# The order of the out-projection products of a seven-product feed-forward block

## The chip, the core and the metric

The kernel runs on one core of a Trainium2 chip. The core's engines work side by side, each through its own stream of instructions in order: TensorE (PE in the profile, with its weight loads as PEld), VectorE (DVE), ScalarE (ACT), GpSimd (POOL) and SyncE (SP), which here only starts transfers. They wait for one another through semaphores. The metric is the device time of one execution in microseconds (us); before the change it was 1460.97 us, the median of three runs (1460.22, 1460.97, 1462.96).

## What is computed

One inference step of a streaming speech encoder with model width 1024, for a prompt of 512 frames and for 8 running streams with 16 new frames each; 640 columns in all. Layer 0 is a convolution module and a feed-forward block, layer 1 is attention over shared keys and values and a second feed-forward block. Everything is float32. The change lies in the feed-forward blocks alone:

```python
def swiglu_ffn(h, g, w_in, w_out):
    a, b = jnp.split(rms_norm(h, g) @ w_in, 2, axis=-1)
    return h + (jax.nn.silu(a) * b) @ w_out
...
for l in range(DEPTH):
    ...
    h = swiglu_ffn(h, norm_ffn[l], w_ffn_in[l], w_ffn_out[l])
```

The hidden width is 2816, that is 22 blocks of 128.

## The kernel before

**Three matmuls for one.** The kernel keeps float32 accuracy by splitting each operand into a rounded part and a residue: `put` (L370) lets ACT copy the value into the high part (L371) and then lets DVE subtract that from the value for the low part (L372). A product of a weight tile and a tile of activations is three matmuls (high by high, low by high, high by low), all issued at L439.

**Seven products for eight.** Both matrix products of the feed-forward block are further cut with the Strassen-Winograd scheme: a 2x2 block product is made of seven products of sums of blocks. The 640 columns are the two halves of 320 (`NH`). For the input projection, `seven` (L524) makes one hidden block with both its columns' halves: it reads weights with `w_seven` (L410), makes seven products, and `gate` (L472) multiplies SiLU of `a` with `b`. Two of its seven products are put off: the function returns `after`, and `after(0)`, `after(1)` run the last products and the block's two gates. `combined` (L488) turns the gates of two neighbouring blocks into the block sums that the output projection needs. The last of their four gates, that of `after(1)` of the second block, makes four of them, named after their product in the table below: `XT2`, `X22`, `XT3` and `XT4`. Each is a gate or a subtraction on DVE (L476, L479, L510, L518), then a copy on ACT, then a residue on DVE.

**Output stretches.** `out_chunk` (L555) is called three times in each of the two feed-forward blocks, after six hidden blocks each time. The six *output stretches* are counted here in order of time: 1 to 3 in layer 0, 4 to 6 in layer 1. A stretch adds six hidden blocks' part of the output to `h`. It has four output row pairs `u` (0 to 3), and seven products for each. A product is three steps of three matmuls, one step for each pair of hidden blocks that it sums over; the third step of products 6, 3, 7 and 4 needs what the very last gate makes. The table of products and their PSUM buffers, and what one call does, are these lines (L557 to L580):

```python
prod = {5: ("e", XT1, True, 1, 1), 1: ("a", X11, True, 0, 0),
        2: ("b", X21, True, 0, 0), 6: ("a", XT2, False, 1, 0),
        3: ("e", X22, False, 1, 0), 7: ("a", XT3, False, 1, 1),
        4: ("a", XT4, False, 0, 1)}
...
    with tc.issue_after(last[0]) if last else nullcontext():
        ins = product(pt, ws[u][x], list(zip(HH[x], HL[x])), first,
                      {"": None, "'": (0, 1), '"': (2,)}[part])
    last[:] = [ins.ins]
    ...
        nc.vector.tensor_tensor(out=hv, in0=hv, in1=pt, op=sub if row else add)
```

Products 1, 6, 7 and 4 of one row pair pile up, in this order, in one PSUM buffer (`a`), products 5 and 3 in another (`e`). After each of them DVE adds the buffer to `h` (L580), and the next product may write the buffer only after that addition has read it.

**The order** of the products is written out by hand in the string `QORD` (L65). A token is product number and row pair: `60` is product 6 of row pair 0. A prime (`60'`) stands for the first two steps, a double prime (`60"`) for the third step, which ends the product and is followed by the addition. `a0` and `a1` are `after(0)` and `after(1)`. `issue_after` keeps the products of PE in this order. The last two products of row pair 3, `73` and `43`, are put between the products of the next call of `seven`. Everything else (the cuts of weights, the gates, the additions) is put in order by the compiler's planner, from its own estimate of when each is ready; on DVE and ACT the planned order is then fixed.

**Weights.** `w_seven(..., True)` is called at the first product of each row pair: one transfer of 768 KB into one of two buffers `raw` (SP, L414), two smaller ones into `s` (POOL, L417 and L418, the second adds to the first), three sums on DVE (L422, L423, L425; L422 is the first that needs `raw`), and seven cuts with `put`, in the order XT1, X11, X21, XT2, X22, XT3, XT4. The cut weights go to eleven slots in turn, so that a cut waits for the product that used the weights cut eleven places before. The cut for product 6 of row pair 2 thus waits for product 4 of row pair 0 (`40`), that for product 1 of row pair 2 for `30`, that for product 2 of row pair 2 for `70`. A `raw` buffer is free when the last of its seven cuts is done, and the transfer of the next `seven` waits for that of row pair 2.

Of the kernel before, what the change touches and what calls it, by code (L numbers as in the profile page):

```python
# [61 lines left out]
X11, X21, XT2, XT1, XT3, XT4, X22 = range(7)  # L62
NCH, CW = 3, 6
HIX = {X11: 0, X21: 1, XT1: 2, XT2: 3, XT3: 4, X22: 5, XT4: 6}
QORD = """50' a0 a1 10' 50" 10" 20 60' 30' 51' 51" 11' 60" 30" 11" 21 70 61 31 40 52 71 12 22 41 62 32 53 72  # L65
          13 23 42 63 33"""
BO = "a0 s0 a1 s1 b0 b1 t0 n0 p0 c0 d0 t1 n1 c1 d1"
BL = "a0 o2 s0 a1 o2 s1 q2 t0 q2 n0 b0 q2 b1 q2 c0 q2 d0 t1 q2 n1 o2 c1 o2 d1 p0 o2"
# [14 lines left out]
def tile_trunk(ctx, tc, xT, vecs, hist, w_pw1, w_pw2, w_in0, w_out0, w_os0, w_in1, w_out1, w_os1,  # L83
# [249 lines left out]
    def ffn(l, w_in, w_out, w_os, tail, hf, lead=(), b0=None, last_sum=()):  # L333
# [221 lines left out]
        def out_chunk(c, HH, HL, after):  # L555
# [26 lines left out]
            last = []  # L582
            for t in QORD.split():
                if t[0] == "a":
# [1103 lines left out]
```

## Time and profile before

| What | Number |
|---|---|
| median of three runs | 1460.97 us |
| profiled execution, its device time | 1461.67 us |
| span in its profile, first to last instruction | 1459.5 us |
| matmuls in the span | 11022, of which 1512 are those of the output stretches |
| TensorE clock granted | 0.999 of full speed |

The profile is one execution, 0.70 us longer than the median. A row of the timeline begins with start and duration in microseconds and ends, where the engine sat idle before it, with that idle time and what ended it. Matmuls overlap: a matmul of 320 columns is shown with 0.31 us, and the next one starts 0.145 to 0.15 us after it started. The starts are therefore what to count with.

### The profile page before, as it was taken

Reading aid. Unit: us, or ns where it says so; the run is one execution under the profiler, and the core shown is the slowest. Engines: PE = TensorE matmul, PEld = TensorE weight load, DVE = VectorE, ACT = ScalarE, POOL = GpSimd, SP = SyncE. Lnnn points to the kernel's source line nnn. Section 1 sums busy time; section 2 is a strip of 40 time slices with the busy share of each in tenths; the row PEclk is TensorE's granted clock in tenths of the full one; section 3 lists DMA queues with packets and bytes.
Section 4 is the critical chain, followed back from the end, with each engine's and each line's share of the span. In section 5 each row is a group of like instructions: output and inputs, shape, how many; then the busy total and the mean of one; then the engine's idle time right before and its main releaser. Section 6 shows DMA issues by size and latency. Waiting matters only on the chain. (4 is left out here: it accounts for less than half of the span.)

```text
span 1459.5 us, 28220 instructions
## 1 busy us (share of the span) xinstructions
PE 1432.7 (98%) x11022; PEld 1369.1 (94%) x11022; DVE 1144.6 (78%) x2520; ACT 758.5 (52%) x1628; POOL 297.5 (20%) x349
## 2 busy tenths in 40 slices
PE   9999999999999999999999999999999999999998
PEld 8998799999999999999987898878999999999998
DVE  6789867988888888756768668577889788879855
ACT  4666554654554554545564355443554464555443
POOL 5699130011111111013222121011001111111101
PEclk9999999999999999999999999999999999999999
DMA  7267434044534444425556554452134543534522
GB/s 243 74 182 187 121 87 145 14 134 150 138 103 140 141 104 121 116 87 194 181 163 214 179 190 159 140 197 72 39 82 128 151 134 89 175 101 106 162 62 72
DMA packets 66932, 192.56 MB, mean 132 GB/s; under 512 B 12144, under 2 KB 30320, under 8 KB 58480
## 3 DMA queue, kind: packets, MB, share of 16 engines
q1 hardware_dynamic: 52432, 160.58, 33.5%
q0 software_dynamic: 13504, 29.37, 10.0%
q8 instruction: 86, 1.41, 0.4%
q10 hardware_dynamic: 864, 0.83, 0.2%
q14 instruction: 46, 0.38, 0.1%
HBM read 179.14 MB, written 11.61 MB: 131 GB/s over the span
## 5 line engine op out<-in xcount | busy, mean ns | idle before, releaser
L439 PE MATMUL mm<-XH,whi 128*128 128x320 f32 x896 | 276.4, 310 | 4.6 <-ACT t L451 4.2
L439 PE MATMUL mm<-XH,wlo 128*128 128x320 f32 x896 | 276.1, 309 | 0.0
L439 PE MATMUL mm<-XL,whi 128*128 128x320 f32 x896 | 273.9, 309 | 0.0
L371 ACT ACTIVATE whi<-raw 128x512 fp32r<-128x512 f32 (+2 forms) x280 | 168.5, 613 | 134.7 <-PE mm L439 113.5
L372 DVE TENSOR_TENSOR wlo<-raw,whi 128x512 fp32r<-128x512 f32 (+2 forms) x280 | 184.3, 667 | 23.4 <-ACT whi L371 21.6
L199 PE MATMUL mm<-xh,whi 128*128 128x320 f32 (+2 forms) x640 | 200.2, 314 | 1.1 <-ACT whi L164 0.8
L200 PE MATMUL mm<-xh,wlo 128*128 128x320 f32 (+2 forms) x640 | 198.2, 311 | 0.0
L201 PE MATMUL mm<-xl,whi 128*128 128x320 f32 (+2 forms) x640 | 195.9, 311 | 0.4 <-DVE xl L189 0.4
L439 PE MATMUL mm<-hid,whi 128*128 128x320 f32 x732 | 171.8, 310 | 2.7 <-DVE h L580 2.7
L439 PEld LDWEIGHTS mm<-XH,whi 128*128 128x128 f32 x896 | 167.8, 188 | 7.0 <-ACT t L451 6.3
L439 PEld LDWEIGHTS mm<-XH,wlo 128*128 128x128 f32 x896 | 168.2, 188 | 0.0
L439 PEld LDWEIGHTS mm<-XL,whi 128*128 128x128 f32 x896 | 167.6, 188 | 0.0
L439 PEld LDWEIGHTS mm<-hid,whi 128*128 128x128 f32 x732 | 125.1, 188 | 4.3 <-DVE h L580 4.3
L199 PEld LDWEIGHTS mm<-xh,whi 128*128 128x128 f32 x640 | 120.5, 188 | 4.4 <-ACT xh L187 1.5
L201 PEld LDWEIGHTS mm<-xl,whi 128*128 128x128 f32 x640 | 119.7, 188 | 1.2 <-DVE xl L189 0.8
L200 PEld LDWEIGHTS mm<-xh,wlo 128*128 128x128 f32 x640 | 120.5, 189 | 0.2
L439 PE MATMUL mm<-hid,wlo 128*128 128x320 f32 x366 | 113.0, 309 | 0.0
L439 PE MATMUL mm<-XH,shi 128*128 128x320 f32 x344 | 106.0, 309 | 1.1 <-ACT t L451 1.1
L439 PE MATMUL mm<-XH,slo 128*128 128x320 f32 x344 | 106.0, 308 | 0.0
L439 PE MATMUL mm<-XL,shi 128*128 128x320 f32 x344 | 105.6, 308 | 0.0
L841 POOL TENSOR_TENSOR ca<-ca,cvt 128x512 f32<-128x512 f32 x60 | 91.9, 1531 | 17.8 <-ACT cvt L838 11.2
L417 POOL DMA_DIRECT2D s<-in_w_in x38 | 22.1, 582 | 355.7 <-DVE wlo L372 142.2
(275 smaller groups left out, 3372.7 us busy)
## 6 DMA issues: line engine op xcount, KB each, us to landing
raw<-in_w_in SPq DMA_DIRECT2D x38, 1024.0 KB
s<-in_w_in POOLq DMA_DIRECT2D x76, 256.0 KB, 4.2
raw<-in_w_os SPq DMA_DIRECT2D x24, 768.0 KB
cache<-in_ck SPq DMA_DIRECT2D x32, 512.0 KB
cache<-in_cv SPq DMA_DIRECT2D x32, 512.0 KB
raw<-in_w_pw SPq DMA_DIRECT2D x11, 1024.0 KB
s<-in_w_os POOLq DMA_DIRECT2D x48, 192.0 KB, 3.7
raw<-in_w_kq SPq DMA_DIRECT2D x8, 1024.0 KB
```

Source lines behind the costliest of these rows:

```text
L199: nc.tensor.matmul(ps, wh, xh, start=(first and i == 0), stop=False)
L200: nc.tensor.matmul(ps, wl, xh, start=False, stop=False)
L201: end = nc.tensor.matmul(ps, wh, xl, start=False, stop=(stop and i == last))
L371: put_end[1] = nc.scalar.activation(out=hi, in_=src, func=AF.Copy).ins
L372: put_end[0] = nc.vector.tensor_tensor(out=lo, in0=src, in1=hi.bitcast(F32), op=sub).ins
L417: nc.gpsimd.dma_start(s1, src[:, 2 * n:3 * n])
L439: last = nc.tensor.matmul(pt, wt, v, start=(first and k == i == 0), stop=(k == n - 1 and i == 2), skip_group_check=True)
L841: nc.gpsimd.tensor_tensor(out=acc, in0=acc, in1=pr, op=ALU.add)
```

## The change

Only the string `QORD` changes. Both orders have the same 26 products (252 matmuls a stretch, with `73` and `43`), the same loads, cuts, gates and additions.

```diff
-QORD = """50' a0 a1 10' 50" 10" 20 60' 30' 51' 51" 11' 60" 30" 11" 21 70 61 31 40 52 71 12 22 41 62 32 53 72
+QORD = """50' a0 a1 10' 50" 10" 20 60' 30' 51' 60" 30" 51" 70 11 21 40 61 31 52 71 12 22 41 62 32 53 72
           13 23 42 63 33"""
```

The third steps `60"` and `30"`, which need what the last gate makes, now stand ahead of `51"` and `11'` (nine matmuls). `70` now stands ahead of all of `11` and of `21`, and is parted from `60"` by `30"` and `51"` (six matmuls) where it was parted by `30"`, `11"` and `21` (fifteen). `40` stands ahead of `61` and `31`, and is parted from `70` by 18 matmuls as before. Product `11` is no longer made in two parts. From `52` on, the order is the former one.

## The prediction

> **What bounds the kernel now.** I read the page first, then the idle time of the matmul line L439, then the timeline of each output stretch.
>
> ```profile
> PE 1432.7 (98%) x11022; PEld 1369.1 (94%) x11022; DVE 1144.6 (78%) x2520; ACT 758.5 (52%) x1628; POOL 297.5 (20%) x349
> L439 PE MATMUL mm<-hid,whi 128*128 128x320 f32 x732 | 171.8, 310 | 2.7 <-DVE h L580 2.7
> ```
>
> PE is busy for 98% of the span. The change keeps every matmul, so it can only move what PE waits for, and in the stretches that is little. The view of line L439 counts it over the whole kernel (weight loads and matmuls together, so a wait can stand twice):
>
> ```profile
>   ACT t L451: 13.1, 20
>   DVE h L580: 12.8, 18
> ```
>
> The waits for `t` come from `seven`, and the change leaves them. Those for `h` are products waiting for an addition. What such a wait costs shows in stretch 2, ahead of `72`:
>
> ```profile
> 462.12 0.31 PE L439 MATMUL mm<-hid,slo 128*128 128x320 f32 x1
> 462.27 0.31 PE L439 MATMUL mm<-hid,shi 128*128 128x320 f32 x1
> 463.56 0.41 PE L439 MATMUL mm<-hid,shi 128*128 128x320 f32 x1 [0.99 <-DVE h L580]
> 463.82 0.31 PE L439 MATMUL mm<-hid,slo 128*128 128x320 f32 x1
> ```
>
> Matmuls start 0.146 us apart (462.12 to 462.27). The waiting one starts 1.29 after its forerunner, 1.14 too late, and the next 0.26 after it, 0.11 too late. So the loss is 1.26, which is the idle time shown plus 0.27. I price the other waits the same way.
>
> **The change part by part.** Nothing is added or removed: no instruction, DMA or buffer. Three things move.
>
> *1. `60"` is asked for nine matmuls earlier: 9 x 0.146 = 1.31 us.* It needs XT2 of the last gate, and its third matmul needs XT2's residue, written by DVE. In each stretch I looked up when that residue is done and when the third matmul runs:
>
> ```profile
> 330.97 0.48 DVE L580 TENSOR_TENSOR h<-h,mm 128x320 f32<-128x320 f32 x1
> 331.36 1.29 DVE L372 TENSOR_TENSOR hid<-B,hid 128x320 fp32r<-128x320 f32 x3
> 331.90 0.41 PE L439 MATMUL mm<-hid,shi 128*128 128x320 f32 x1
> 443.04 0.89 DVE L372 TENSOR_TENSOR hid<-B,hid 128x320 fp32r<-128x320 f32 x2
> 443.84 0.48 DVE L580 TENSOR_TENSOR h<-h,mm 128x320 f32<-128x320 f32 x1
> 444.23 0.31 PE L439 MATMUL mm<-hid,whi 128*128 128x320 f32 x1
> 556.62 0.88 DVE L372 TENSOR_TENSOR hid<-B,hid 128x320 fp32r<-128x320 f32 x2
> 557.71 0.31 PE L439 MATMUL mm<-hid,whi 128*128 128x320 f32 x1
> 1113.96 0.48 DVE L580 TENSOR_TENSOR h<-h,mm 128x320 f32<-128x320 f32 x1
> 1114.36 1.29 DVE L372 TENSOR_TENSOR hid<-B,hid 128x320 fp32r<-128x320 f32 x3
> 1114.90 0.41 PE L439 MATMUL mm<-hid,shi 128*128 128x320 f32 x1
> 1226.56 0.88 DVE L372 TENSOR_TENSOR hid<-B,hid 128x320 fp32r<-128x320 f32 x2
> 1227.76 0.46 PE L439 MATMUL mm<-hid,whi 128*128 128x320 f32 x2
> 1338.25 0.89 DVE L372 TENSOR_TENSOR hid<-B,hid 128x320 fp32r<-128x320 f32 x2
> 1339.44 0.31 PE L439 MATMUL mm<-hid,whi 128*128 128x320 f32 x1
> ```
>
> The first residue of each merged row is XT2's, 0.48 to 0.49 long. In stretch 1 it ends at 331.85 and the matmul starts 0.05 later: it was waiting for it already. In stretch 2 it is ready at 443.04 + 0.49 + 0.05 = 443.58 and used at 444.23, a slack of 0.65. Asked for 1.31 earlier, the matmul waits 1.31 - 0.65 + 0.11 = 0.77. Stretch 3 has 0.56 slack, hence 0.86; stretch 6 has 0.65, hence 0.77; stretch 5 has 0.67, hence 0.75. In stretches 1 and 4 the whole 1.31 would be lost, but there the addition just ahead of the residue (330.97, 1113.96) is that of `51"`, which now comes later. The residue moves up by that row's 0.40 us start to start, so 0.91 each. Sum of the six: **+4.97 us**. Behind the waiting matmul stand `30"`, `51"` and all further products, since PE's order is fixed. If DVE keeps its old order in stretches 1 and 4 too, the sum is 5.8. If the planner moves XT2's residue ahead of a weight cut, it is less (third rival).
>
> *2. `70` follows `60"` after six matmuls, 0.87 us, in place of fifteen.* Both write buffer `a`, so the addition of `60"` must be done in between. After XT2's residue DVE has two more, 0.40 us each start to start, then can take the addition. In stretch 2: with `51"`'s addition gone (443.84), XT4's residue takes that place, the addition of `60"` runs 444.24 to 444.72, and `70` is wanted at 443.58 + 0.25 + 0.87 = 444.70. It waits 0.07 + 0.11 = 0.18. One weight cut ahead of the addition in some stretches would add about 0.5 there; none is in the way if the addition goes first. I take 0.25 a stretch: **+1.50 us**. The nearest pair of the old order is `10"` and `60'`, also in one buffer, nine matmuls apart:
>
> ```profile
> 327.29 0.42 PE L439 MATMUL mm<-hid,shi 128*128 128x320 f32 x1 [0.57 <-DVE h L580]
> 553.34 0.42 PE L439 MATMUL mm<-hid,whi 128*128 128x320 f32 x1 [0.31 <-DVE h L580]
> 1110.29 0.41 PE L439 MATMUL mm<-hid,shi 128*128 128x320 f32 x1 [0.99 <-DVE h L580]
> 439.23 0.48 DVE L580 TENSOR_TENSOR h<-h,mm 128x320 f32<-128x320 f32 x1
> ```
>
> Three stretches lose 0.84, 0.58 and 1.26 there. In stretch 2 the addition ends at 439.71 for a product wanted at 439.98, 0.22 in hand with the 0.05. With six matmuls instead of nine, 0.44 less room, this gives 1.28 + 1.02 + 1.70 and 0.33 for each of the three others: 5.0 us. That is the upper end; the lower is 0.
>
> The Trainium skill, Perfetto Trace Analysis, Optimizing Tensor Performance, says that independent matmul groups should rotate through PSUM banks so that one group's evacuation lies beside the next group's matmuls. It speaks against this move, which puts two products of one bank closer; taken by itself it would set the upper end just worked out, and the three rows agree with it in three stretches of six.
>
> *3. `40` is done 18 matmuls, 2.63 us, earlier against the end of the group (ahead of `52`).* The chain that hangs on it ends in the wait shown first:
>
> ```profile
> 451.71 0.46 PE L439 MATMUL mm<-hid,whi 128*128 128x320 f32 x2
> 452.05 0.94 ACT L371 ACTIVATE whi<-raw 128x384 fp32r<-128x384 f32 x2 [0.74 <-PE mm L439]
> 453.60 0.55 DVE L372 TENSOR_TENSOR wlo<-raw,whi 128x384 fp32r<-128x384 f32 x1
> 454.17 0.33 SPq L414 DMA_DIRECT2D raw<-in_w_in  x1
> 462.42 0.69 DVE L422 TENSOR_TENSOR raw<-raw 128x512 f32<-128x512 f32 x1 [2.34 <-DMA raw<-in_w_in]
> 463.03 0.48 DVE L580 TENSOR_TENSOR h<-h,mm 128x320 f32<-128x320 f32 x1
> ```
>
> The first row is the last matmul of `40`, ending 0.31 later at 452.02, with the first of `52`. ACT cuts the weights whose slot `40` held, DVE ends the row pair's last cut at 454.15, SP issues the next weights' transfer at 454.17. L422 waits for it on DVE for 2.34 us, and the addition of `62`, long ready, stands behind L422 at 463.03 with `72` behind it at 463.56. The other stretches that wait there:
>
> ```profile
> 350.68 0.42 PE L439 MATMUL mm<-hid,whi 128*128 128x320 f32 x1 [0.30 <-DVE h L580]
> 576.98 0.42 PE L439 MATMUL mm<-hid,whi 128*128 128x320 f32 x1 [0.92 <-DVE h L580]
> 1134.17 0.41 PE L439 MATMUL mm<-hid,whi 128*128 128x320 f32 x1 [0.25 <-DVE h L580]
> 1358.42 0.42 PE L439 MATMUL mm<-hid,whi 128*128 128x320 f32 x1 [0.63 <-DVE h L580]
> 1119.10 0.41 PE L439 MATMUL mm<-hid,whi 128*128 128x320 f32 x1 [0.27 <-DVE h L580]
> ```
>
> With 0.27 each, `72` costs 0.57, 1.26, 1.19, 0.52, 0 and 0.90: 4.44 us. In the new order PE reaches `72` about 1.0 us later by parts 1 and 2, and the transfer is issued up to 2.63 - 1.0 = 1.6 us sooner on the clock. In stretch 2 `72` is then wanted at 463.4 and its addition is done by 462. Even a transfer that lands no sooner leaves only 0.1 there. I take all **-4.44 us**. The last row is `61` of stretch 4, waiting for the addition of the first product; `61` now comes 18 matmuls later, so **-0.54 us**. What `61` and `31` release for row pair 3 comes 1.3 us later, but eight products, 10.5 us, lie between `61` and `53`, the first to need it.
>
> Sum: 4.97 + 1.50 - 4.44 - 0.54 = **+1.5 us**. The profiled execution, 1461.67, would be 1463.2; as it lies 0.7 above the median, I predict on the median: 1460.97 + 1.5 = **1462.5 us**. I count on 0.2% (2.9 us) as what a measurement tells from no change, so the forecast is within it.
>
> **The rivals.**
>
> *`70` takes over the wait (slower).* DVE reaches the addition of `60"` behind gate residues and weight cuts, as it reached that of `10"`. For it: the three rows of `60'`, and a DVE that is busy for 7.94 of 8.00 us from 444 on in stretch 2 (the first row under the last rival). Against: DVE is then past the gate. It decides once the addition ends over 0.3 us after `70` is wanted. With 5.0 in place of 1.5 the sum is +5.0: **1466.0**.
>
> *The transfer isn't earlier (slower).* If DVE's backlog holds the last cut so that the transfer moves with PE, the waits at `72` stay: 4.97 + 1.50 - 0.54 = +5.9, **1466.9**. Against: the 2.15 us from the end of `40` (452.02) to the issue are a plain chain, with `40` at its head.
>
> *The gate's residue comes sooner (faster).* DVE takes XT2's residue well after ACT's copy. If the planner puts it two places earlier in stretches 2, 3, 5 and 6, their front waits (3.15) vanish: -1.7, 1459.3. If `70` doesn't wait either, -3.2: **1457.8**. Against: nothing that DVE does before that residue gets later there, so the planner has no reason.
>
> *The clock gives way.* More short gaps could lower PE's clock.
>
> ```profile
> 444.00:452.00 8.00, 8.00 (x56) 8.00 (x55) 7.94 (x19) 3.52 (x7) 0.57 (x1) 1.00 0.34 118
> 429.00:475.00 46.00, 44.49 (x302) 43.96 (x301) 1.00 0.49 142
> ```
>
> Both rows are of the windows view, the first with busy time of all engines (PE, PEld, DVE 7.94 of 8.00, ACT, POOL), the second with that of L439 alone (PE, PEld); the granted clock stands third from the end. It is 1.00 across stretch 2, whose gaps reach 0.99 us. A product of nine at half speed after each of six gaps would add 6 x 1.31 = 7.9 to the sum: 1470.4. The Trainium skill, TensorE: Matmul & The Clock Gate, A second HAM failure mode, tells of a kernel whose micro-idles between matmul groups made the clock swing between half and full; the trace disagrees for gaps of this size.
>
> **How the numbers follow.** Forecast, with the milder third rival (within 0.2%): 0.56. `70` takes over 0.20, transfer not earlier 0.12, clock 0.01, others slower 0.01: slower 0.34. Third rival in full: faster 0.10. The range leaves out half of the faster case and about a tenth at the top: 1458.3 to 1467.0, which takes in both slower rivals.
>
> **What would show it.** Right: in all six stretches the third matmul of `60"` waits for a residue (L372), 0.8 to 0.9 us; no wait ahead of `72`; the transfer after `40` 1 to 2 us earlier; `61` of stretch 4 free. Wrong: `70` idle over 0.3 us behind L580; L422 still idle for over 2 us with an addition that PE needs behind it; or XT2's residue at another place in DVE's order, which would change every term of part 1.

## The result and the profile after

The changed kernel takes 1460.57 us, the median of 22 runs (1457.96 to 1463.17). The kernel before takes 1463.14 us on the same chip, also the median of 22 (1460.05 to 1467.13). The ratio is 0.998 [0.9973, 0.9988]: the change made the kernel 2.6 us faster where 1.5 us slower had been forecast. On two later occasions, on another chip, the changed kernel again took 1460.7 and 1460.8 us, but the kernel before took only 1460.8 both times. The changed kernel's time is settled; the gain is between nothing and 0.2%. The forecast of 1462.5 us stood on a base of three runs, 1460.97, which is 2.2 us below the median of 22; shifted by that, the forecast range would only just hold the measured time.

The profiled execution of the changed kernel took 1461.79 us, with a span of 1460.0, against 1461.67 and 1459.5 before. The totals show nothing of the change: first the busy time of the engines, then the costliest PE group with `hid` (busy, mean ns, idle time ahead of it and its releaser).

```profile
span 1460.0 us, 28194 instructions
PE 1434.0 (98%) x11022; PEld 1369.6 (94%) x11022; DVE 1138.9 (78%) x2520; ACT 757.8 (52%) x1628; POOL 297.6 (20%) x349
L439 PE MATMUL mm<-hid,whi 128*128 128x320 f32 x732 | 172.5, 311 | 5.5 <-DVE hid L372 3.1
```

The view of the idle time ahead of line L439 does (us in total, times):

```profile
  DVE hid L372: 9.7, 12
  DVE h L580: 8.1, 18
  ACT t L451: 6.7, 12
```

Residues (L372) now head it, 9.7 us in 12 pieces, which are the six stretches counted for PE and for the weight loads; before, they stood at 0.7 in 2. Waits for additions fell from 12.8 to 8.1. The waits for `t`, which the prediction said the change leaves, fell from 13.1 to 6.7. The timeline of PE's waits says which products these are. The third matmul of `60"` in the six stretches, waiting for XT2's residue:

```profile
331.67 0.42 PE L439 MATMUL mm<-hid,shi 128*128 128x320 f32 x1 [0.48 <-DVE hid L372]
444.43 0.56 PE L439 MATMUL mm<-hid,whi 128*128 128x320 f32 x2 [0.54 <-DVE hid L372]
558.13 0.42 PE L439 MATMUL mm<-hid,whi 128*128 128x320 f32 x1 [1.02 <-DVE hid L372]
1113.75 0.42 PE L439 MATMUL mm<-hid,shi 128*128 128x320 f32 x1 [0.48 <-DVE hid L372]
1227.42 0.55 PE L439 MATMUL mm<-hid,whi 128*128 128x320 f32 x2 [1.02 <-DVE hid L372]
1339.59 0.41 PE L439 MATMUL mm<-hid,whi 128*128 128x320 f32 x1 [0.54 <-DVE hid L372]
```

In stretches 1 and 4 the first matmul of the step also waits, for ACT's copy (0.28 and 0.26 idle). Counted as start to start time over 0.146 us, as in the prediction, PE loses in the stretches:

| us lost ahead of | before | after | forecast difference | measured difference |
|---|---|---|---|---|
| `60"` (XT2 of the last gate) | 0.72 | 6.78 | +4.97 | +6.06 |
| `70` (addition of `60"`) | 0 | 1.07 | +1.50 | +1.07 |
| `72` (addition of `62`) | 4.46 | 0 | -4.44 | -4.46 |
| `61` of stretch 4 | 0.54 | 0 | -0.54 | -0.54 |
| XT4 product of the last `seven` (`t`) | 5.24 | 1.60 | 0 | -3.64 |
| `40` (addition of `70`) | 0 | 1.72 | 0 | +1.72 |
| `62` (addition of `12`) | 0 | 1.03 | 0 | +1.03 |
| `60'` (addition of `10"`) | 2.68 | 2.60 | 0 | -0.08 |
| sum | 13.64 | 14.81 | +1.5 | +1.2 |

The sum is nearly the forecast one, but its parts are not, and that it comes so close is luck: four rows were forecast with the right sign, three that were not forecast move 6.4 us between them and mostly cancel. The two profiled executions differ by +0.12 in device time and by +0.5 in span.

**The move that the diff doesn't show.** The timeline of PE at the start of stretch 2, before and then after:

```profile
432.44 0.30 PE L439 MATMUL mm<-XL,shi 128*128 128x320 f32 x1
433.27 0.42 PE L439 MATMUL mm<-XH,shi 128*128 128x320 f32 x1 [0.53 <-ACT t L451]
```

```profile
433.16 0.30 PE L439 MATMUL mm<-XL,shi 128*128 128x320 f32 x1
433.31 0.31 PE L439 MATMUL mm<-hid,whi 128*128 128x320 f32 x1
...
434.04 0.31 PE L439 MATMUL mm<-hid,whi 128*128 128x320 f32 x1
434.19 0.31 PE L439 MATMUL mm<-XH,shi 128*128 128x320 f32 x1
```

In both, the first row is the last matmul of the XT3 product in the last `seven`. Its result is copied out of PSUM by ACT (`keep`, L451), and `a0`, the XT4 product, writes the same buffer and waits for that copy. Before, `a0` follows directly and loses 0.80 us. After, the six matmuls of `50'` (0.87 us) lie in between and the copy is done. The token `50'` stands first in both orders, but it is the one product of the string that `issue_after` ties to nothing (`last` is empty at the start), so the planner may put it ahead of the XT3 product or behind it. For the new string it put it behind in stretches 2, 3, 5 and 6, ahead in 1 and 4. Why a string that differs only from 69 matmuls later on tips this choice isn't shown by any run. The products of the next `seven` are tied to nothing either, and they moved too (between `42` and `63` lie 3 of their matmuls in every stretch, where in four there were 7), but PE waits at none of them.

Of the 3.64 us in the row of `t`, four times 0.80 go with this move. The other 0.45 is in stretch 4, where `50'` stays and the wait was 1.26 and is 0.81; the same kernel before has 1.19 there in a second profile (e6).

**The wait that the earlier transfer was to remove, and where its like turned up.** Rows of DVE and PE after, with the wait ahead of `40` in stretch 1 and that ahead of `62` in stretch 2:

```profile
335.00 0.56 DVE L422 TENSOR_TENSOR raw<-raw 128x384 f32<-128x384 f32 x1 [2.19 <-DMA raw<-in_w_os]
335.95 0.88 DVE L580 TENSOR_TENSOR h<-h,mm 128x320 f32<-128x320 f32 x2
337.21 0.48 DVE L580 TENSOR_TENSOR h<-h,mm 128x320 f32<-128x320 f32 x1
337.75 0.42 PE L439 MATMUL mm<-hid,whi 128*128 128x320 f32 x1 [0.65 <-DVE h L580]
...
458.87 0.69 DVE L422 TENSOR_TENSOR raw<-raw 128x512 f32<-128x512 f32 x1 [1.20 <-DMA raw<-in_w_in]
459.95 0.48 DVE L580 TENSOR_TENSOR h<-h,mm 128x320 f32<-128x320 f32 x1
460.58 0.39 PE L439 MATMUL mm<-hid,whi 128*128 128x320 f32 x1 [0.16 <-DVE h L580]
```

The mechanism is the one that the prediction read off for `72`: L422 waits on DVE for a transfer, additions stand behind it, and a product stands behind the addition. Before, it struck `72`. After, the transfer for the next `seven` lands ahead of `72`'s need, but late enough to hold `62` by a little; and in stretches 1 and 4 it is L422 of row pair 3, waiting for its own transfer (2.19 and 2.07 us, where it was 0.64 and 1.18). It stood ahead of the addition of `70` before, too, but now `70` comes sooner, and `40` needs that addition.

### The profile page after: what moved, and what is told of

The parts are those of the page before. It is cut to its first block, busy times and chain, and to the rows that moved or that the text cites. A ratio compares the mean times of both kernels' runs of the same rounds, so it can differ in the third digit from the quotient of the medians.

```text
span 1460.0 us, 28194 instructions
## 1 busy us (share of the span) xinstructions
PE 1434.0 (98%) x11022; PEld 1369.6 (94%) x11022; DVE 1138.9 (78%) x2520; ACT 757.8 (52%) x1628; POOL 297.6 (20%) x349
## 5 line engine op out<-in xcount | busy, mean ns | idle before, releaser
L439 PE MATMUL mm<-XH,whi 128*128 128x320 f32 x896 | 275.9, 310 | 2.9 <-ACT t L451 2.6
L439 PE MATMUL mm<-XH,wlo 128*128 128x320 f32 x896 | 276.1, 309 | 0.0
L439 PE MATMUL mm<-XL,whi 128*128 128x320 f32 x896 | 274.5, 309 | 0.0
L372 DVE TENSOR_TENSOR wlo<-raw,whi 128x512 fp32r<-128x512 f32 (+2 forms) x280 | 183.9, 666 | 15.9 <-ACT whi L371 14.8
L439 PE MATMUL mm<-hid,whi 128*128 128x320 f32 x732 | 172.5, 311 | 5.5 <-DVE hid L372 3.1
L439 PEld LDWEIGHTS mm<-XH,whi 128*128 128x128 f32 x896 | 167.7, 188 | 4.9 <-ACT t L451 4.2
L439 PEld LDWEIGHTS mm<-XH,wlo 128*128 128x128 f32 x896 | 168.2, 188 | 0.0
L439 PEld LDWEIGHTS mm<-XL,whi 128*128 128x128 f32 x896 | 167.7, 188 | 0.0
L439 PEld LDWEIGHTS mm<-hid,whi 128*128 128x128 f32 x732 | 125.0, 188 | 8.8 <-DVE hid L372 4.2
L439 PE MATMUL mm<-hid,wlo 128*128 128x320 f32 x366 | 113.0, 309 | 0.0
L439 PE MATMUL mm<-XH,slo 128*128 128x320 f32 x344 | 106.0, 308 | 0.0
L439 PE MATMUL mm<-XH,shi 128*128 128x320 f32 x344 | 105.8, 309 | 0.0
L439 PE MATMUL mm<-XL,shi 128*128 128x320 f32 x344 | 105.6, 308 | 0.0
```

The costliest lines, as they stand in the source:

```text
L372: put_end[0] = nc.vector.tensor_tensor(out=lo, in0=src, in1=hi.bitcast(F32), op=sub).ins
L439: last = nc.tensor.matmul(pt, wt, v, start=(first and k == i == 0), stop=(k == n - 1 and i == 2), skip_group_check=True)
```

## The experiments

The theory after the result: the new order by itself costs a few microseconds, as forecast, and the planner's move of `50'` gives back 3 to 4. The rivals: `50'` doesn't matter, and the gain comes from the earlier transfer; or the front is harmless and the cost lies elsewhere. The first four kernels cross the two orders with the two places of `50'` and take one cause of `72`'s wait away without touching the order.

**e1: the old order, `50'` held behind the XT3 product.** Two of three changed lines:

```diff
-            xproduct(pa, ws[XT3], XT3, False)
+            xt3[0] = xproduct(pa, ws[XT3], XT3, False).ins
...
-            last = []
+            last = [xt3[0]]
```

> The old order, with product 50' tied behind the XT3 product of the last seven in all six stretches (the planner put it there in four stretches of the changed kernel, and ahead of that product in the kernel before). Nothing else moves but a few DVE instructions. Theory A (half of the gain or more is 50' now filling PE's wait for t ahead of a0): the wait for t of 0.80 us goes in six stretches, 1.25 in the fourth, so 5.2 us less on PE, of which the waits ahead of 72 may take back some: ratio 0.9965 to 0.9985. Theory B (the gain is the transfer chain behind 40 alone): what is won ahead of the stretch is lost again at 72, ratio 0.9995 to 1.0005.

Measured: 1458.67 us against 1461.46, ratio 0.9986 [0.9975, 0.9998]. In the trace the waits for `t` fall from 5.24 to 1.13 us, which is 4.1; what stays is the XT3 product, which now waits itself, 0.57 in stretches 1 and 4. The time falls by only 2.8, just short of Theory A's range: in this trace `72` loses 5.77 instead of 4.46, `60'` 3.8 instead of 2.68 and `61` 0.9 instead of 0.54. Of the loss at `72`, 3.87 is one wait in stretch 3, dearer than idle time and restart explain; the last section comes back to it.

**e2: the old order, L422 of the next `seven` behind the addition of `62`.**

```diff
-                        nc.vector.tensor_tensor(out=a21, in0=a11, in1=a21, op=add)
+                        with behind(*(() if out else add62)):
+                            nc.vector.tensor_tensor(out=a21, in0=a11, in1=a21, op=add)
...
+                if (i, u) == (6, 2):
+                    add62[:] = [end.ins]
```

> The old order, with the DVE sum L422 of the next seven, which waits for its weights' transfer, tied behind the addition of 62. On each engine only this instruction changes its place, past one addition, in six stretches. It prices the wait ahead of 72 by itself. Theory A and B: the wait ahead of 72 (4.4 us in the profile of before) goes, ratio 0.996 to 0.998; if the profile of before showed that wait shorter than most executions have it, more than 4.4 us. If 72's wait was covered by something else that is late as well, ratio 0.999 to 1.

Measured: 1457.48 us, ratio 0.998 [0.9967, 0.9993]. Rows of DVE in stretch 2 (line numbers are one higher here):

```profile
460.28 0.48 DVE L581 TENSOR_TENSOR h<-h,mm 128x320 f32<-128x320 f32 x1
461.07 0.69 DVE L423 TENSOR_TENSOR raw<-raw 128x512 f32<-128x512 f32 x1 [0.30 <-DMA raw<-in_w_in]
```

The addition of `62` now goes ahead of the sum that waits, and PE loses nothing ahead of `72` in any stretch. In stretch 5 the transfer takes 8.45 us from issue to use, longer than in any stretch of before, and `72` doesn't wait there either. So a late transfer alone doesn't make `72` wait; it takes L422's place ahead of the addition in DVE's fixed order as well.

**e3: the new order, `50'` held ahead of the XT3 product**, as the planner has it in the old order.

```diff
-            xproduct(pa, ws[XT3], XT3, False)
+            with tc.issue_after(mid()) if mid else nullcontext():
+                xproduct(pa, ws[XT3], XT3, False)
...
+            def head():
+                go(5, 0, "'")
+                return last[0]
```

> The new order, with product 50' back ahead of the XT3 product in all six stretches, as in the kernel before. Theory A: the wait for t of 0.8 us is back in four stretches, 3.2 us more than the changed kernel, ratio to the kernel before 0.9995 to 1.001. Theory B: as the changed kernel, 0.9975 to 0.9985.

Measured: 1464.59 us, ratio 1.0021 [1.001, 1.0033]. This is the change that the prediction reckoned with, and it is 3.1 us slower than before, more than Theory A had expected. Idle time ahead of L439:

```profile
  ACT t L451: 12.0, 20
  DVE h L581: 10.1, 17
  DVE hid L372: 8.3, 12
```

The waits for `t` are back (4.79 us lost), those for the residue stay (6.05).

**e4: the new order, `50'` behind the XT3 product in all six stretches** (the edit of e1).

> The new order, with product 50' behind the XT3 product in all six stretches, not in four. Theory A: another 1.6 us less than the changed kernel, ratio to the kernel before 0.9965 to 0.9975. Theory B: as the changed kernel, 0.9975 to 0.9985.

Measured: 1460.88 us, ratio 0.9992 [0.9981, 1.0004], the changed kernel's own time; neither theory's range held it. Moving `50'` in stretches 1 and 4 as well brings next to nothing, since the XT3 product waits 0.57 there, as in e1. From e3 to e4, of the products only `50'` moves: 3.7 us of time, and 3.7 us less lost for `t` in the traces (4.79 to 1.13). That settles the theory's second half. The four kernels, beside one another on one chip, give the new order a price of 3.1 us with `50'` early and 2.2 with it late, and the move of `50'` a gain of 2.8 in the old order and 3.7 in the new.

**e5, e6, e12: the changed kernel and the kernel before once more.**

> The changed kernel once more, unaltered, beside the following ones on one chip. Theory A (the products' order by itself costs 3 us, 50' in the wait for t gives 3 to 4 back, and before loses more at 72 in most executions than in its profile): ratio to the kernel before 0.998 to 0.9995. Its profile shows no wait at 72 and the wait for t in the first and fourth stretch only.

> The kernel before, unaltered, for a second profile. Theory A: the loss ahead of 72 hangs on when a transfer lands and differs from execution to execution; this profile shows it at 4 to 8 us in the sum of the six stretches, unlike the first by 1 us or more, while the waits for t (5.2 us) are the same. Rival: all waits are as in the first profile within 0.5 us.

> The changed kernel unaltered a third time. Its ratio to before was 0.998 in the first measurement and 0.9995 in the second, on different chips. Theory A: the changed kernel takes about the same everywhere (1460 to 1461 us) and before differs with the landing of its transfers, so the ratio lies between 0.998 and 1 and before's median between 1460.5 and 1463.5.

Measured: the changed kernel 1460.71 us (11 runs), ratio 0.9995 [0.9986, 1.0003], and 1460.81 (11 runs), ratio 0.9996 [0.9985, 1.0007]. The first comparison's 0.998 isn't met again. What differs is the kernel before: 1463.14 us there, 1461.46 beside e1 to e4, 1460.79 and 1460.76 here. Its profile on this chip (e6: 1460.47 us) shows where it can vary. PE loses 11.48 us in the stretches instead of 13.64. `72` loses 1.70 instead of 4.46, well under the 4 to 8 expected, and `61` 0.9 more:

```profile
455.98 0.33 SPq L414 DMA_DIRECT2D raw<-in_w_in  x1
462.56 0.69 DVE L422 TENSOR_TENSOR raw<-raw 128x512 f32<-128x512 f32 x1 [0.67 <-DMA raw<-in_w_in]
```

The transfer in stretch 2 is used 6.58 us after its issue, where it was 8.25 (454.17 to 462.42, rows of the prediction), and `72` doesn't wait. So the old order's time hangs on when a transfer lands, the new order's hardly does. That fits a gain that differs from chip to chip. Why one occasion differs from another isn't shown, so it stays open.

**e7: e1 and e2 together. e8: in addition, L422 of row pair 2 in stretches 1 and 4 behind the addition of `10"`, and L422 of row pair 3 behind that of `11"`.** The core of e8's edit:

```diff
+SUMS = {(1, 0): 2, (1, 1): 3, (6, 2): 4}
...
+                        with behind(*sums.get(u, ())):
+                            nc.vector.tensor_tensor(out=a21, in0=a11, in1=a21, op=add)
...
+                if (i, u) in SUMS and (c == 0 or u):
+                    sums[SUMS[i, u]] = [end.ins]
```

> The old order with both: 50' behind the XT3 product, and L422 of the next seven behind the addition of 62. Theory A: both gains, 4.1 us of t and 4.4 us or more of 72, ratio 0.9945 to 0.9965. If one covers the other: that of the better one alone, 0.9975 to 0.9985.

> As the one before, and L422 of row pair 2 in the first and fourth stretch behind the addition of 10", L422 of row pair 3 behind that of 11": no addition that PE waits for stands behind a sum that waits for a transfer. Theory A: the waits of 60' in the first and fourth stretch (0.84 and 1.26 us in the profile of before) and of 61 in the fourth (0.54) go too, about 2 us less than the one before, ratio 0.993 to 0.9955. Rival: as the one before.

Measured: e7 1456.85 us, ratio 0.9966 [0.9953, 0.9978], at the weak end of what was expected; e8 1453.57 us, ratio 0.9948 [0.9934, 0.9963]. Both beat both kernels, and keep the old order. Idle time ahead of the matmul line in e8 (L441 there):

```profile
  DVE h L583: 7.5, 8
  ACT t L453: 6.0, 12
  DVE hid L373: 3.2, 4
```

Additions cost 7.5 in 8 pieces instead of 12.8 in 18. But e8's profiled run, 1456.96 us, is not e8's median (its six runs reach from 1451.96 to 1458.03), and the losses in it (8.08 us) are no smaller than e7's (6.95). The intervals of e7 and e8 overlap, too, so the step from e7 to e8 is neither certain nor explained.

**e9: the front alone; e10: `40` early without the front.** Against the order of e3, with `50'` held early in both:

```diff
-50' a0 a1 10' 50" 10" 20 60' 30' 51' 60" 30" 51" 70 11 21 40 61 31 52
+50' a0 a1 10' 50" 10" 20 60' 30' 51' 60" 30" 51" 11 21 70 61 31 40 52
...
+50' a0 a1 10' 50" 10" 20 60' 30' 51' 51" 11' 60" 30" 11" 70 21 40 61 31 52
```

> One part of the change alone: 60" and 30" ahead of 51" and 11, then 21 70 61 31 40 as in the old order; 50' held ahead of the XT3 product, as before. Theory A: 60" waits for the gate, 5.3 us more than before in the six stretches, and the transfer behind 40 moves with it, so that little of it is taken back: ratio 1.002 to 1.004. Rival (the waits ahead of 72 absorb what PE loses earlier): 0.9995 to 1.001.

> The other part alone: 51" and 11' stay ahead of 60" and 30", then 11" 70 21 40 61 31; 50' held ahead of the XT3 product, as before. Theory A: no wait at 60" beyond the 0.7 us of before, the transfer for the next seven issued some 2.6 us sooner and landing in 5 to 6 us, no wait ahead of 72 (-4.5 us), up to 2 us of waits at 70 and 40, where additions follow closer or stand behind a sum: ratio 0.997 to 0.9995. Rival (the earlier 40 is worth nothing by itself): 0.9995 to 1.001.

Measured: e9 1477.51 us, ratio 1.0111 [1.0096, 1.0126]; e10 1465.93, ratio 1.0031 [1.0018, 1.0044]. Both are slower than either theory expected. Idle time ahead of L439 in e9 (in e10 additions cost 20.6 in 22 pieces):

```profile
  DVE h L581: 24.1, 21
  ACT t L451: 12.0, 20
  DVE hid L372: 8.3, 12
```

In e9 `60"` loses what it loses in e3 (6.08 and 6.05), and `72` loses 11.89 instead of 4.46. PE's delay at the front did not let the transfer catch up, since `40`, the head of its chain, was delayed as much. Of the growth of 7.43, about 3.9 is landing (8.05 us on the mean of six from issue to use, 7.40 before), about 1.5 a slowed clock in stretch 4 (last section); 2.0 are not settled. In e10 `72` never waits, but `40` loses 7.03, and behind it in stretch 1 a slowed clock costs another 1.5. In stretch 2:

```profile
451.01 0.48 DVE L581 TENSOR_TENSOR h<-h,mm 128x320 f32<-128x320 f32 x1
451.55 0.42 PE L439 MATMUL mm<-hid,whi 128*128 128x320 f32 x1 [0.69 <-DVE h L581]
```

`40` follows `70`, whose buffer it shares, by nine matmuls there instead of 18, and the addition between them stands behind cuts and sums. So neither half is better than the whole: +16.8 and +5.2 us, where both together cost 3.1 (e3). e10 is no clean half, though: it puts `70` and `40` nine matmuls apart, which neither the old order nor the new one does, and most of its loss at `40` goes with that (7.03, where e3 has 2.1).

**e11: the new order with all that helped the old one** (`50'` late, L422 behind the additions of `10"`, `70` and `62`).

```diff
+SUMS = {(1, 0): 2, (7, 0): 3, (6, 2): 4}
```

> The new order with 50' behind the XT3 product and the three sums behind the additions of 10", 70 and 62. Theory A: the waits at 60" (6.3 us) and 70 (1.1) stay, those of t (1.6), 40 (1.7 to 2.4) and 62 (1.0) go: 4 us less than the changed kernel, ratio to the kernel before 0.9965 to 0.998, and 3 us or more slower than the same in the old order (0.9948). Rival (with the sums out of the way the order of the products no longer matters): 0.994 to 0.996.

Measured: 1457.61 us, ratio 0.9979 [0.9969, 0.999]. In its trace `60"` loses 7.49 us, `70` 1.07, `t` 1.13, `60'` 1.28, and nothing else anything. With the other waits out of the way, the new order is 4.0 us slower than the old one (e8, 1453.57, six runs). By the traces the main part of that is the price of asking for the last gate's output early: `60"` loses 7.49 here and 2.67 in e8.

## Why the prediction was wrong, step by step

**The step that failed** is what the prediction says first of the change, "Nothing is added or removed: no instruction, DMA or buffer. Three things move", with "The waits for `t` come from `seven`, and the change leaves them". A fourth thing moved, `50'`, six matmuls past the XT3 product in four stretches, and with it 3.2 us of waits for `t` went (3.64 with what stretch 4 lost less for another reason). The prediction saw that wait, 13.1 us in the first view it quotes, and set it aside because its line isn't in the diff. It also saw that the planner orders what isn't tied, but applied that to DVE alone ("the planner has no reason"). e3 shows the change as it was reckoned with: +3.1 us [1.5, 4.8 from the interval of the ratio], where +1.5 was forecast. e4, with `50'` late in all six, shows the missing step: -3.7. Together they leave next to nothing (e4, -0.6), which is also what the two later comparisons found; the -2.6 of the first has more in it than this step.

**`60"` waits in all six stretches: right, and too small by 1.09.** The mechanism was as told. Stretches 1 and 4 lose 0.95 and 0.91 more than before where 0.91 was worked out, stretches 2 and 6 0.81 where it was 0.77. Stretches 3 and 5 lose 1.29 instead of 0.86 and 0.75. In both DVE had waited for a transfer of this stretch's weights at L422, 1.43 and 0.96 us, and came late to all that stands behind it, the addition that `60'` needs and XT2's residue. Stretch 3:

```profile
550.78 0.56 DVE L422 TENSOR_TENSOR raw<-raw 128x384 f32<-128x384 f32 x1 [1.43 <-DMA raw<-in_w_os]
...
553.92 0.41 PE L439 MATMUL mm<-hid,whi 128*128 128x320 f32 x1 [0.73 <-DVE h L580]
...
557.60 1.29 DVE L372 TENSOR_TENSOR hid<-B,hid 128x320 fp32r<-128x320 f32 x3
558.13 0.42 PE L439 MATMUL mm<-hid,whi 128*128 128x320 f32 x1 [1.02 <-DVE hid L372]
```

In e5, the same kernel with the same order on DVE, L422 doesn't wait in stretch 3, and `60"` loses 0.81 there, as in stretches 2 and 6, where it doesn't wait either. The prediction took the residue's time from one profile of before, in which L422 of stretch 3 waited as well (1.58) and the residue was still in time. It didn't ask how much of such a wait the new order could bear.

**`70` takes over the wait: no.** It loses 0.18 in each stretch, 1.07 in all, beside 1.50 forecast and 5.0 at the upper end. 0.18 is exactly what was worked out for stretch 2 (0.07 + 0.11); the allowance for a weight cut in between wasn't needed, since DVE takes the addition directly behind the three residues (445.10 in stretch 2). The Trainium skill, Perfetto Trace Analysis, Optimizing Tensor Performance, asks to rotate groups through PSUM banks. For this pair the trace doesn't bear out a cost of closeness beyond those 0.18; for `70` and `40` in e10, nine matmuls apart, it does: 7.03. What differs between the two is what stands on DVE ahead of the addition: nothing but residues for the first, cuts and sums for the second. How close the products are doesn't tell it by itself.

**`72` no longer waits: right**, all 4.46. In stretch 2 the transfer is issued at 453.35, 0.82 earlier than before, less than the 1 to 2 us that were to be seen. L422 starts at 458.87, 3.55 earlier, because the transfer also lands sooner after its issue (5.52 us, 8.25 before). At 8.25 L422 would start at 461.60, and `62`, whose addition stands behind it, would by that reckoning wait 2.7 us longer. The term was right with part of its reason missing.

**`61` of stretch 4: right**, -0.54.

**Priced at nothing and not nothing:** `40` (+1.72) and `62` (+1.03). The prediction followed L422 of the next `seven` into `72` and didn't ask which additions stand behind *each* L422 once the products that need them come sooner. `40` was said to be parted from `70` by 18 matmuls as before; what DVE has to do in these 18 was not counted.

**The clock rival: right that it doesn't act here**, with 1.00 granted across all six stretches of the changed kernel. Its mechanism exists, though: e1, e9 and e10 show it at longer gaps.

**What stays open.** The waits sum to +1.2 in the one pair of profiles. Device time outside the span is 1.8 to 1.9 us in every run of the changed kernel and 2.1 to 2.2 in every one of before, some 0.3 less. Neither gives -2.6, the first comparison's difference, nor do the two later comparisons, which found none. The kernel before differs by 2.4 us between occasions, which is more than the change does to it.

## What to carry to other kernels

When a planner orders what isn't tied by hand, a reordering can move instructions that the diff doesn't name: list every product that is tied to nothing, and price both of its places. In an engine that works in order, ask for each instruction that waits for a transfer what stands behind it and who needs that; putting six such sums behind one addition each was worth 0.2%, and with the rest of e8 0.5%, with the string as it was. Half of a reordering can cost more than the whole, so a half that is tested alone has to be checked for waits that neither full order has.

## What the runs showed of the hardware

**A 1 MB transfer landed sooner in the new order.** Issues on SP and POOL in stretch 2, before and then after:

```profile
452.99 0.85 POOL L418 DMA_DIRECT2D s<-in_w_in  x1 [2.99 <-DVE h L580]
454.17 6.27 SPq L414 DMA_DIRECT2D raw<-in_w_in  x2
454.31 0.57 POOL L417 DMA_DIRECT2D s<-in_w_in  x1 [0.47 <-issue]
```

```profile
453.35 10.10 SPq L414 DMA_DIRECT2D raw<-in_w_in  x2
453.56 0.85 POOL L418 DMA_DIRECT2D s<-in_w_in  x1 [3.04 <-DVE wlo L372]
456.76 0.57 POOL L417 DMA_DIRECT2D s<-in_w_in  x1 [2.35 <-issue]
```

In the old order POOL issues two transfers close to the 1 MB one of SP (L414), one 1.18 us before it and one 0.14 us after it, and L422 starts 6.1 to 8.2 us after SP's issue (before and e6, twelve stretches), up to 9.4 in e1. In the new order one stands close, 0.21 us after it, and the other comes 3.4 us after it; L422 then starts after 5.3 to 5.5 us (after, six stretches), 5.0 to 5.7 over e3, e4, e5, e10 and e12. One neighbour beside the transfer is thus compatible with the short time. That two neighbours get in its way is argued from this; no kernel moved only one of them.

**A gap of about 2 us can halve the clock for 3.4 us, and its place on a fixed grid matters.** In e1, stretch 3, `72` starts after 2.15 us idle, and its matmuls then start 0.266 us apart instead of 0.146. The windows view of L439 there (length, PE busy and count, PEld, granted clock, DMA share, GB/s):

```profile
577.00:578.00 1.00, 0.25 (x1) 0.25 (x2) 0.79 0.96 227
578.00:579.00 1.00, 1.00 (x5) 1.00 (x6) 0.50 0.80 148
579.00:580.00 1.00, 1.00 (x5) 1.00 (x5) 0.50 0.06 10
580.00:581.00 1.00, 1.00 (x5) 1.00 (x5) 0.51 0.00 0
581.00:582.00 1.00, 1.00 (x9) 1.00 (x8) 1.00 0.00 0
```

A granted 0.79, 0.50, 0.50 and 0.51 is half speed for 0.42 + 1 + 1 + 0.98 = 3.4 us, which costs 1.45 of that wait's 3.87. The same happened for 3.4 us after a gap of 2.06 in e10 and of 1.87 in e9, but not after one of 2.36 in e9, nor after one of 1.73 in e6. The clock's own records show a grid: in e9 half speed begins at 30.36, 1143.10 and 1470.78 us, the second and third 326 and 422 steps of 3.4133 us after the first. Counted back from 1143.10 by such steps, the gap of 2.36 (353.40 to 355.76) is cut at 354.63 into 1.23 and 1.13 us. The three gaps that halved the clock have 1.97 (e1), 2.06 and 1.87 us within one step, and half speed begins with the next step; the 1.73 of e6 also lie within one. That the idle time within one step decides is inferred from these five gaps. It isn't idle time alone: around 29 us, long before the stretches, nine of the fourteen traces show half speed for 3.41 us behind a gap of only 1.2, and no run here tells what else counts.

The Trainium skill, TensorE: Matmul & The Clock Gate, What's actually happening, tells of a free-running window of 3413 ns and of half rate; the length and the grid agree. From its advice to avoid idle gaps over some 3 us (Why this matters for your kernels) the trace differs: three gaps of 1.87 to 2.15 us were enough.
